# The V chunk of the differential heads projected before the other heads' q and k, in a hybrid attention layer

## Chip, cores and metric

The kernel runs on one core of a Trainium2 chip. The metric is the device time of one execution in microseconds (us), the median of several runs of the same program.

## What is computed

One decoder layer for 256 tokens of width 1024, all in float32. One input projection gives q, k and v of two groups of heads: four differential heads (two softmaxes each, the second subtracted with a weight) and eight block-sparse heads, which at 256 tokens see one causal block each. One output projection mixes both, then follow a layer norm, a SwiGLU feed-forward and a second layer norm.

```
proj = x @ w_in
dq, dk, dv, mq, mk, mv = split(proj)          # 512 columns each
# differential heads: q, k as 4 heads x 2 x 64, v as 4 heads x 128
p = softmax(causal(rope(dq) @ rope(dk).T / 8))
a = p[:, :, 0] - lam * p[:, :, 1]
o = a @ dv;  o = o * rsqrt(mean(o*o) + eps) * subln_g * (1 - lambda_init)
# the other 8 heads of 64: one block of 256, its own
b = softmax(causal(rope(mq) @ rope(mk).T / 8)) @ mv
x = layer_norm(alpha * x + concat(o, b) @ w_o)
f = (silu(g) * u) @ w_ffn_out                 # g, u = split(x @ w_ffn_in)
x = layer_norm(alpha * x + f)
```

## The kernel before

Each product of two float32 matrices is made of three matmuls on rounded parts: a matrix is split into `hi` (a cast on ScalarE, line 108) and `lo` (what is left, a subtraction on VectorE, line 109), and `mm3` (line 155) adds hi*hi, hi*lo and lo*hi. Weights come in units of 128 x 4 x 512 (four blocks of 512): units 0 to 11 are the six chunks of the input projection, two units each, 12 to 15 the output projection, then the feed-forward. A unit is loaded whole or in parts by SyncE into one of four raw buffers, and split into one of four hi and four lo buffers. `spread` (line 126) lays the splits of coming units over the steps of a projection, in `pieces` parts a unit: at 4, one block of 512 at a time.

The chunks stand in the order q and k of the differential heads (0, 1), q and k of the other heads (2, 3), V of the differential heads (4), V of the others (5). `proj_qkT` (line 422) makes a q or k chunk transposed, in 32 steps of three matmuls of 256 columns; at the end of a chunk's first half `rope` rotates it (a shuffle, two products, later an addition and the split, `finish`), at the end of its second half `plain` splits the rest. `proj_v` (line 454) makes a V chunk in 16 steps of three matmuls of 512 columns and copies it out on ScalarE.

Other work is hooked onto steps of the projections; the tables of lines 38 to 40 name the steps. `scores(g, b)` (line 305) makes the scores of four heads into four PSUM banks, then reduces them on VectorE (line 319) and takes the exponentials on ScalarE (line 322). `diff_combine` (line 336) subtracts the two softmaxes on VectorE (line 344), `diff_pt` transposes the result on TensorE and copies it on ScalarE, `diff_pv` (line 350) multiplies with V and normalises: VectorE (line 365), eight squares on ScalarE (line 367), a power on GpSimd (line 370), VectorE (line 371). `diff_mix` transposes that into the first half of `mixh`, `mixl`. For the other heads `norm1` and `moba_norm` scale the exponentials (VectorE and ScalarE), `moba_pt` transposes them, `moba_pv` multiplies with V and fills the second half. `wo(t, n, half)` (line 500) is a quarter of the output projection over one half of the mix, 12 matmuls of 512 columns. Behind the attention the buffers are closed, and GpSimd's queue loads the norm's rows (`load_rows`, line 527) into the space that comes free.

Before, the two scores of group 0 are hooked into chunk 2 (steps 15 and 28), the combine into chunk 3 (step 12), its transposes into chunk 3 (steps 22, 25, 28, 31), the scores of group 1 into chunk 4 (steps 5 and 11). Chunk 5 carries `diff_pv` (step 4), `norm1` (5), six of the eight `moba_pt` (8 to 13) and both `diff_mix` (12 and 14).

A hook is the earliest place in program order, not a fixed one. A planner walks the program when it is built, with times of its own, and puts on each engine's queue the first instruction in program order that it takes to be ready; on the chip each queue then runs in that order and waits where an input is late. `run` (line 293) also puts VectorE's instructions of a hook behind the last reduction of the scores traced so far.

## Time and profile before

| | |
|---|---|
| median of 3 runs | 309.2 us (309.18 to 309.55) |
| the profiled execution | 309.19 us |
| its span in the trace | 307.4 us |
| TensorE busy | 296.7 us, 97% of the span |
| VectorE busy | 246.6 us, 80% |
| ScalarE busy | 181.2 us, 59% |
| DMA | 57.25 MB, mean 186 GB/s |

The span runs from the first instruction to the last; 1.8 us of the execution lie around it. A busy share is a mean over stages: here the attention with its projections (up to about 118 us) is one part and the feed-forward the rest. An engine that is marked busy may still be held inside an instruction, so starts are compared with starts.

### The profile page before, as it was taken

Reading aid. Unit: us, or ns where it says so; the run is one execution under the profiler, and the core shown is the slowest. Engines: PE = TensorE matmul, PEld = TensorE weight load, DVE = VectorE, ACT = ScalarE, POOL = GpSimd, SP = SyncE. Lnnn points to the kernel's source line nnn. Section 1 sums busy time; section 2 is a strip of 40 time slices with the busy share of each in tenths; the row PEclk is TensorE's granted clock in tenths of the full one; section 3 lists DMA queues with packets and bytes.
Section 4 is the critical chain, followed back from the end, with each engine's and each line's share of the span. In section 5 each row is a group of like instructions: output and inputs, shape, how many; then the busy total and the mean of one; then the engine's idle time right before and its main releaser. Section 6 shows DMA issues by size and latency. Waiting matters only on the chain.

```text
span 307.4 us, 4877 instructions
## 1 busy us (share of the span) xinstructions
PE 296.7 (97%) x1835; PEld 254.4 (83%) x1835; DVE 246.6 (80%) x460; ACT 181.2 (59%) x349; POOL 9.0 (3%) x18
## 2 busy tenths in 40 slices
PE   8999999899999999999999999999999999999990
PEld 5899998878886888888888888888888888888890
DVE  3697999977684489849598797598768999997995
ACT  4684888587994326357466567547747746557000
POOL 1000000000110011000000000000000000000011
PEclk9999999999999999999999999999999999999997
DMA  6988984345359243529554664574470365824011
GB/s 187 338 271 270 418 341 146 135 148 194 122 201 310 116 139 128 199 85 330 216 160 141 247 194 140 215 241 151 156 245 31 107 211 194 309 91 184 0 68 68
DMA packets 14390, 57.25 MB, mean 186 GB/s; under 512 B 1760, under 2 KB 2784, under 8 KB 9632
## 3 DMA queue, kind: packets, MB, share of 16 engines
q1 hardware_dynamic: 14080, 54.86, 51.6%
q0 software_dynamic: 288, 2.10, 1.7%
q8 instruction: 14, 0.23, 0.3%
q14 instruction: 8, 0.07, 0.1%
HBM read 55.90 MB, written 1.05 MB: 185 GB/s over the span
## 4 chain that ended last, share of the span: by engine, by line
PE 88%; DVE 6%; DMA 2%; SPq 1%; issue 1%; ACT 0%; DVEq 0%
PE fc L681 22%; PE foc L757 12%; PE fc L682 11%; PE pj L156 6%; PE pj L158 6%; PE pj L157 6%; PE fo L757 5%; PE wo L156 3%; PE fr L157 2%; PE fr L156 2%; PE wo L157 2%; PE wo L158 2%; PE fr L158 2%; DMA xTr<-in_xT_dram 2%; DVE lo L109 2%; PE s L314 2%
## 5 line engine op out<-in xcount | busy, mean ns | idle before, releaser
L109 DVE TENSOR_TENSOR lo<-raw,hi 128x512 fp32r<-128x512 f32 (+2 forms) x114 | 104.0, 938 | 21.4 <-ACT hi L108 21.1
L108 ACT CAST hi<-raw 128x512 fp32r<-128x512 f32 (+2 forms) x114 | 88.9, 824 | 21.5 <-PE wo L158 9.9
L681 PE MATMUL fc<-x1T,hi 128*128 128x512 f32 x288 | 100.1, 392 | 0.0
L682 PE MATMUL fc<-x1T,lo 128*128 128x256 f32 x288 | 80.5, 280 | 0.0
L681 PEld LDWEIGHTS fc<-x1T,hi 128*128 128x128 f32 x288 | 54.1, 188 | 11.9
L682 PEld LDWEIGHTS fc<-x1T,lo 128*128 128x128 f32 x288 | 54.0, 188 | 0.0
L156 PE MATMUL pj<-xTh,hi 128*128 128x256 f32 x128 | 36.5, 292 | 0.1
L158 PE MATMUL pj<-xTh,lo 128*128 128x256 f32 x128 | 36.0, 286 | 0.3
L157 PE MATMUL pj<-xTl,hi 128*128 128x256 f32 x128 | 36.0, 283 | 0.0
L684 ACT COPY v<-fc 128x256 f32<-128x256 f32 x36 | 13.3, 368 | 22.0 <-PE fc L682 21.9
L156 PEld LDWEIGHTS pj<-xTh,hi 128*128 128x128 f32 x128 | 24.3, 192 | 1.4 <-ACT hi L218 1.2
L158 PEld LDWEIGHTS pj<-xTh,lo 128*128 128x128 f32 x128 | 24.1, 190 | 1.2 <-DVE lo L220 0.8
L157 PEld LDWEIGHTS pj<-xTl,hi 128*128 128x128 f32 x128 | 24.3, 190 | 0.0
L685 DVE TENSOR_TENSOR v<-v,fc 128x256 f32<-128x256 f32 x36 | 15.0, 417 | 6.2 <-ACT v L684 6.2
L757 PE MATMUL foc<-lo,hTh 128*128 128x512 f32 x46 | 18.2, 395 | 0.0
L757 PE MATMUL foc<-hi,hTh 128*128 128x512 f32 x46 | 18.1, 394 | 0.0
L757 PE MATMUL foc<-hi,hTl 128*128 128x512 f32 x46 | 18.1, 394 | 0.0
L322 ACT ACTIVATE E<-E,negm 128x128 f32<-128x128 f32 (+1 forms) x32 | 14.1, 443 | 4.3 <-DVE negm L319 4.3
L156 PE MATMUL pj<-hi,xTh 128*128 128x512 f32 x32 | 13.5, 422 | 0.0
L156 PE MATMUL wo<-hi,mixh 128*128 128x512 f32 x32 | 12.9, 404 | 0.0
L688 ACT ACTIVATE v<-v 128x256 f32<-128x256 f32 x18 | 7.5, 419 | 9.1 <-DVE v L685 9.1
L156 PE MATMUL fr<-hi,x1T 128*128 128x512 f32 x32 | 12.9, 402 | 0.0
(190 smaller groups left out, 517.9 us busy)
## 6 DMA issues: line engine op xcount, KB each, us to landing
raw<-in_w_f_dram SPq DMA_DIRECT2D x27, 1024.0 KB, 5.1
raw<-in_w_in_dram SPq DMA_DIRECT2D x24, 256.0 KB, 6.0
raw<-in_w_in_dram SPq DMA_DIRECT2D x4, 1024.0 KB, 8.2
raw<-in_w_o_dram SPq DMA_DIRECT2D x4, 1024.0 KB, 4.8
raw<-in_w_f_dram SPq DMA_DIRECT2D x12, 256.0 KB, 3.7
raw<-in_w_f_dram SPq DMA_DIRECT2D x6, 512.0 KB, 4.5
raw<-in_w_in_dram SPq DMA_DIRECT2D x4, 512.0 KB, 7.3
rows<-in_rows_dram POOLq DMA_DIRECT2D x2, 1024.0 KB, 6.4
```

The costliest lines, as they stand in the source:

```text
L108: nc.scalar.copy(h, src)
L109: nc.vector.tensor_sub(l, src, h.bitcast(F32))
L156: nc.tensor.matmul(ps, sh, mh, start=first, stop=False)
L157: nc.tensor.matmul(ps, sh, ml, start=False, stop=False)
L158: nc.tensor.matmul(ps, sl, mh, start=False, stop=last)
L322: nc.scalar.activation(e, e, AF.Exp, bias=negm[g][:, i, u : u + 1], scale=-1.0, accum_out=ls[g][:, i, u : u + 1])
L681: nc.tensor.matmul(ps, hi[u][:, i, ws], x1T[:, k], start=k == 0, stop=False)
L682: nc.tensor.matmul(ps[:, 0, :], lo[u][:, i, ws], x1T[:, k, 0, :], start=False, stop=k == KT - 1)
L684: nc.scalar.copy(v, ps[:, 1, :])
L685: nc.vector.tensor_add(v, v, ps[:, 0, :])
L688: nc.scalar.activation(gate, gate, AF.Silu)
L757: nc.tensor.matmul(bank[name] if ps is None else ps, x, w[:, cs], start=key not in opened, stop=last and (m, i) == (len(todo) - 1, 2))
```

## The change

The V chunk of the differential heads (4) now stands third: chunks 0, 1, 4, 2, 3, 5. The units are numbered in that order. Its projection carries the two scores of group 0 (steps 7 and 14) and the finish of k's rotation. Chunk 2 carries the combine (step 20) and its own rotation's finish (24, before 31). Chunk 3 carries the differential transposes (2, 5, 8, 11) and `diff_pv` (24). Chunk 5 carries both `diff_mix` (0 and 1) and the scores of group 1 (4 and 10). `norm1` with its scalings and all eight `moba_pt` stand behind chunk 5, between quarters of the output projection; the third quarter, `wo(1, 0, 0)`, moves ahead of the last two `moba_pv`. In `spread`, units of chunks 4 and 5 and of the output projection go in 2 pieces (two blocks at a time), those of q and k in 4.

```diff
--- before.py
+++ after.py
@@ -35,9 +35,12 @@
 SPLIT_PIECES = {16: 4, 17: 4, 18: 4, 19: 4}
 
 
-FIN0, FIN1, FIN2, FIN3 = (20, 26), (4, 7), 31, 20
-SCORES0, SCORES1 = (15, 28), (5, 11)
-COMBINE, DIFF_PT = 12, (22, 25, 28, 31)
+FIN0, FIN1, FIN2, FIN3 = (20, 26), (2, 4), 24, 20
+SCORES0, SCORES1 = (7, 14), (4, 10)
+COMBINE, DIFF_PT, DIFF_PV = 20, (2, 5, 8, 11), 24
+
+
+ORDER = (0, 1, 4, 2, 3, 5)
 
 
 
@@ -68,7 +71,7 @@
 
 
     units = []
-    for c in range(6):
+    for c in ORDER:
         for h in range(2):
             units.append(w_in[c, :, 4 * h : 4 * h + 4, :])
     for u in range(4):
@@ -99,7 +102,7 @@
 
     def split(u, r, s):
         h, l = hi[u][:, s, :], lo[u][:, s, :]
-        if u < 8:
+        if u < 12 and ORDER[u // 2] < 4:
 
             src = r[:, s, :].rearrange("p i (h t d) -> p i t h d", t=2, d=32)
             h, l = (v.rearrange("p i (t h d) -> p i t h d", t=2, d=32) for v in (h, l))
@@ -125,12 +128,14 @@
 
     def spread(units_, pieces, steps):
 
-        gens = [(u, p) for u in units_ for p in range(pieces)]
+
+        pieces = {u: pieces if u < 12 and ORDER[u // 2] < 4 else 2 for u in units_}
+        gens = [(u, p) for u in units_ for p in range(pieces[u])]
         live = {}
 
         def emit(u):
             if u not in live:
-                live[u] = split_gen(u, pieces)
+                live[u] = split_gen(u, pieces[u])
                 state["split"] = u + 1
             next(live[u])
 
@@ -415,7 +420,7 @@
 
 
     def proj_tok(ps, c, t, k):
-        u, i = 2 * c + k // 4, k % 4
+        u, i = 2 * ORDER.index(c) + k // 4, k % 4
         ts_ = slice(t * P, (t + 1) * P)
         mm3(ps, xTh[:, k, ts_], xTl[:, k, ts_], hi[u][:, i, :], lo[u][:, i, :], k == 0, k == KT - 1)
 
@@ -426,14 +431,15 @@
         kb = {0: 1, 1: 4}.get(c, KT)
         order = [(j, k0 + k) for k0 in range(0, KT, kb) for j in range(4) for k in range(kb)]
         fin = []
-        ahead(2 * c, splits=-1)
-        bg = spread([1] + [2] if c == 0 else [3, 4, 5] if c == 1 else [2 * c + 2, 2 * c + 3], 4, 28)
+        u0 = 2 * ORDER.index(c)
+        ahead(u0, splits=-1)
+        bg = spread([1] + [2] if c == 0 else [3, 4, 5] if c == 1 else [u0 + 2, u0 + 3], 4, 28)
         for n, (j, k) in enumerate(order):
             if n == 16:
-                ahead(2 * c + 1, splits=-1)
+                ahead(u0 + 1, splits=-1)
             for f in side.get(n, []) + bg.get(n, []):
                 run(f)
-            u, i = 2 * c + k // 4, k % 4
+            u, i = 2 * ORDER.index(c) + k // 4, k % 4
             ws = slice(j * P, (j + 1) * P)
             ps = pss[j][:, 0, :] if c < 2 else pss[j // 2][:, j % 2, :]
             mm3(ps, hi[u][:, i, ws], lo[u][:, i, ws], xTh[:, k, :], xTl[:, k, :], k == 0, k == KT - 1)
@@ -454,11 +460,12 @@
     def proj_v(c, side):
 
         pss = [psA.tile([P, 512], F32, tag="acc", name=f"pj{c}_{t}") for t in range(2)]
-        ahead(2 * c, splits=-1)
-        bg = spread([2 * c + 2, 2 * c + 3], 4, 14)
+        u0 = 2 * ORDER.index(c)
+        ahead(u0, splits=-1)
+        bg = spread([u0 + 2, u0 + 3], 4, 14)
         for n, (t, k) in enumerate((t, k) for t in range(2) for k in range(KT)):
             if n == 8:
-                ahead(2 * c + 1, splits=-1)
+                ahead(u0 + 1, splits=-1)
             for f in side.get(n, []) + bg.get(n, []):
                 run(f)
             proj_tok(pss[t], c, t, k)
@@ -473,26 +480,28 @@
     sc = {FIN1[i]: [f] for i, f in enumerate(fin)}
     for b in range(2):
         sc.setdefault(SCORES0[b], []).append(lambda b=b: scores(0, b))
-    proj_qkT(2, sc)
-    sc = {COMBINE: [diff_combine]}
+    proj_v(4, sc)
+    proj_qkT(2, {COMBINE: [diff_combine]})
+    sc = {}
     for h in range(4):
         sc.setdefault(DIFF_PT[h], []).append(lambda h=h: diff_pt(h))
+    od = {}
+
+    def run_diff_pv():
+        od["o"] = diff_pv()
+
+    sc[DIFF_PV] = [run_diff_pv]
     proj_qkT(3, sc)
     alloc_group(1)
-    proj_v(4, {SCORES1[b]: [lambda b=b: scores(1, b)] for b in range(2)})
-    od = {}
-
-    def run_diff_pv():
-        od["o"] = diff_pv()
+    sd = {i: [lambda i=i: diff_mix(i, od["o"][i])] for i in range(2)}
+    for b in range(2):
+        sd[SCORES1[b]] = [lambda b=b: scores(1, b)]
+    proj_v(5, sd)
 
     def norm1():
         nc.vector.reciprocal(rl[1], ls[1])
-
-    sd = {4: [run_diff_pv], 5: [norm1] + [lambda u=u: moba_norm(u) for u in range(8)],
-          12: [lambda: diff_mix(0, od["o"][0])], 14: [lambda: diff_mix(1, od["o"][1])]}
-    for n, u in enumerate(range(6)):
-        sd.setdefault(8 + n, []).append(lambda u=u: moba_pt(u))
-    proj_v(5, sd)
+        for u in range(8):
+            moba_norm(u)
 
 
     acc = [[psA.tile([P, 512], F32, tag="acc", name=f"wo{t}_{n}") for n in range(2)] for t in range(2)]
@@ -505,12 +514,16 @@
             mm3(acc[t][n], mixh[:, e, ts_], mixl[:, e, ts_], hi[u][:, i, :], lo[u][:, i, :], e == 0, e == 7)
 
     ahead(12, splits=3)
+    run(norm1)
     wo(0, 0, 0)
+    for u in range(4):
+        moba_pt(u)
+    wo(0, 1, 0)
     moba_pv(0)
-    moba_pt(6)
-    moba_pt(7)
     moba_pv(1)
-    wo(0, 1, 0)
+    for u in range(4, 8):
+        moba_pt(u)
+    wo(1, 0, 0)
     moba_pv(2)
     moba_pv(3)
     axT.close()
@@ -567,7 +580,6 @@
         nc.scalar.copy(x1T_h[:, ks, ts_], pt)
         nc.vector.tensor_sub(x1T_l[:, ks, ts_], pt, x1T_h[:, ks, ts_].bitcast(F32))
 
-    wo(1, 0, 0)
     ahead(12)
     wo(0, 0, 1)
     ln_part("a", 0, 0, x_sb, acc[0][0])
```

## Rows read from the trace of the kernel before

**Rows 1.** The page: part 1, busy time of the engines; part 4, the chain by engine.

```profile
PE 296.7 (97%) x1835; PEld 254.4 (83%) x1835; DVE 246.6 (80%) x460; ACT 181.2 (59%) x349; POOL 9.0 (3%) x18
...
PE 88%; DVE 6%; DMA 2%; SPq 1%; issue 1%; ACT 0%; DVEq 0%
```

**Rows 2.** Table by stage; columns: us, PE, PEld, DVE, ACT, POOL busy (x), PEclk, DMA, GB/s.

```profile
29.90:45.20 15.30, 15.30 (x195) 14.70 (x194) 15.23 (x49) 12.77 (x37) 0.00 (x0) 1.00 0.98 401
45.20:59.80 14.60, 13.07 (x110) 12.70 (x110) 14.60 (x44) 10.20 (x31) 0.00 (x0) 1.00 0.43 145
59.80:74.40 14.60, 14.60 (x146) 11.80 (x145) 10.74 (x43) 11.31 (x41) 0.00 (x0) 1.00 0.41 145
74.40:91.10 16.70, 16.70 (x99) 14.24 (x98) 12.38 (x26) 16.51 (x46) 2.48 (x2) 1.00 0.47 156
91.10:103.90 12.80, 12.80 (x76) 9.52 (x75) 5.20 (x8) 4.83 (x9) 0.71 (x1) 1.00 0.80 290
```

**Rows 3.** Timeline, PE, chunk 3; columns: start us, us, engine, line, op, tiles, form, idle.

```profile
52.75 0.28 PE L157 MATMUL pj<-xTl,hi 128*128 128x256 f32 x1
52.87 0.28 PE L158 MATMUL pj<-xTh,lo 128*128 128x256 f32 x1
...
54.67 0.30 PE L327 MATMUL ppd<-ident,E 128*128 128x128 f32 x1 [1.52 <-DVE E L344]
...
56.57 0.36 PE L156 MATMUL pj<-xTh,hi 128*128 128x256 f32 x1
56.77 0.27 PE L157 MATMUL pj<-xTl,hi 128*128 128x256 f32 x1
```

**Rows 4.** Timeline, VectorE, 39 to 57 us: first softmax, reciprocal, the combine.

```profile
39.75 0.29 DVE L319 CUSTOM_DVE_ANT_0 E<-s,mask 128x128 f32<-128x128 f32 x1
...
41.99 0.74 DVE L270 STREAM_SHUFFLE sh<-pj 128x512 f32<-128x512 f32 x1
...
52.05 0.24 DVE L339 RECIPROCAL rl<-ls 128x16 f32<-128x16 f32 x1
...
54.19 2.70 DVE L344 SCALAR_TENSOR_TENSOR E<-E,sc 128x128 f32<-128x128 f32 x8
```

**Rows 5.** Timeline, PE, the first eight matmuls of the two scores of group 0.

```profile
38.12 0.51 PE L314 MATMUL s<-h,h 32*128 32x256 f32 x8
...
41.74 0.87 PE L314 MATMUL s<-h,h 32*128 32x256 f32 x8
```

**Rows 6.** Timeline, ScalarE: first and last instruction of the second score's exponentials.

```profile
45.95 0.40 ACT L322 ACTIVATE E<-E,negm 128x128 f32<-128x128 f32 x1 [0.16 <-DVE negm L319]
...
49.38 0.19 ACT L322 ACTIVATION_READ_ACCUMULATOR E<-E,negm 128x1 f32 x1
```

**Rows 7.** Timeline, VectorE, pieces of weights: four of 512 and two of 1024 in a row.

```profile
67.22 2.49 DVE L109 TENSOR_TENSOR lo<-raw,hi 128x512 fp32r<-128x512 f32 x4
...
92.88 2.36 DVE L109 TENSOR_TENSOR lo<-raw,hi 128x1024 fp32r<-128x1024 f32 x2 [0.64 <-ACT hi L108]
```

**Rows 8.** Timeline, VectorE, the second half of the differential output, from dpv to od.

```profile
80.07 0.69 DVE L365 TENSOR_TENSOR od<-dpv,rl 128x512 f32<-128x512 f32 x1 [0.83 <-PE dpv L358]
...
86.97 0.69 DVE L371 TENSOR_TENSOR od<-od,ff 128x512 f32<-128x512 f32 x1 [1.13 <-POOL ff L370]
```

**Rows 9.** Timeline, ScalarE: scaling of seven E, two copies of transposes, two casts of 1024.

```profile
76.79 2.90 ACT L386 ACTIVATE E<-E,rl 128x256 f32<-128x256 f32 x7
...
85.27 0.84 ACT L331 COPY ptm<-ppm 128x384 f32<-128x384 f32 x2
...
91.80 2.00 ACT L108 CAST hi<-raw 128x1024 fp32r<-128x1024 f32 x2
```

**Rows 10.** Waits: engine, what, released by: us in total, times, longest us.

```profile
POOL rows L529 <- PE ppm L329: 9.1, 1, 9.1
```

**Rows 11.** The page, part 6: DMA, engine op xcount, KB, us from issue to landing.

```profile
rows<-in_rows_dram POOLq DMA_DIRECT2D x2, 1024.0 KB, 6.4
```

**Rows 12.** Timeline, VectorE: first step of the layer norm that reads the rows.

```profile
111.35 1.40 DVE L555 SCALAR_TENSOR_TENSOR x<-z,mva,rows 128x512 f32<-128x512 f32 x2
```

More of the change, by code (lines that the diff above doesn't have):

```diff
@@ L475, in hybrid_layer_kernel @@
         sc.setdefault(SCORES0[b], []).append(lambda b=b: scores(0, b))
-    proj_qkT(2, sc)
-    sc = {COMBINE: [diff_combine]}
+    proj_v(4, sc)
+    proj_qkT(2, {COMBINE: [diff_combine]})
+    sc = {}
     for h in range(4):
         sc.setdefault(DIFF_PT[h], []).append(lambda h=h: diff_pt(h))
-    proj_qkT(3, sc)
-    alloc_group(1)
-    proj_v(4, {SCORES1[b]: [lambda b=b: scores(1, b)] for b in range(2)})
     od = {}
@@ L486, in run_diff_pv @@
         od["o"] = diff_pv()
+    sc[DIFF_PV] = [run_diff_pv]
+    proj_qkT(3, sc)
+    alloc_group(1)
+    sd = {i: [lambda i=i: diff_mix(i, od["o"][i])] for i in range(2)}
+    for b in range(2):
+        sd[SCORES1[b]] = [lambda b=b: scores(1, b)]
+    proj_v(5, sd)
     def norm1():
         nc.vector.reciprocal(rl[1], ls[1])
-    sd = {4: [run_diff_pv], 5: [norm1] + [lambda u=u: moba_norm(u) for u in range(8)],
-          12: [lambda: diff_mix(0, od["o"][0])], 14: [lambda: diff_mix(1, od["o"][1])]}
-    for n, u in enumerate(range(6)):
-        sd.setdefault(8 + n, []).append(lambda u=u: moba_pt(u))
-    proj_v(5, sd)
+        for u in range(8):
+            moba_norm(u)
     acc = [[psA.tile([P, 512], F32, tag="acc", name=f"wo{t}_{n}") for n in range(2)] for t in range(2)]
```

## Prediction

> **What bounds the kernel now.** I read the page first. TensorE is busy 97% of the span, and the chain that ended last is TensorE for 88%, VectorE for 6% [rows 1]. So nothing that merely makes VectorE or ScalarE lighter counts; only time in which TensorE's queue stands still counts. The table by stage tells where that can be: the stretch 45.2 to 59.8 us, which is chunk 3, is the only one in which TensorE is not busy throughout (13.07 of 14.60), and VectorE is busy there without a break, as in the stage ahead of it (15.23 of 15.30) [rows 2]. The timeline names the place. Matmuls of 256 columns start every 0.12 us; the one at 52.87 should be followed at 52.99, but the first transpose of the differential heads starts at 54.67, released by the combine on VectorE: **1.68 us** [rows 3]. On VectorE the combine began only at 54.19, although the reciprocal that it needs was done at 52.3 and the exponentials ahead of it at 49.6 [rows 4, 6]: it stood behind other work. A smaller wait lies in the second score of group 0: its first eight matmuls take 0.87 us where the first score's took 0.51, so 0.36 us for PSUM banks that the first softmax still holds [rows 5]. The other large stall of the trace is the start, which the change doesn't touch. TensorE's work itself stays: the same matmuls in another order. About 2.0 us are thus to be had in this part, and the rest of the forecast is what the new order puts in their place.
>
> **The wait at the combine.** Before, 10 steps of chunk 3 (3.6 us at three matmuls of 0.12) lie between combine and first transpose; after, 14 steps (12 of chunk 2, two of chunk 3, 5.0 us). The rotation of a q or k chunk, six passes of about 0.6 us on VectorE (one is the 0.74 at 41.99 [rows 4]), no longer stands between the two softmaxes of group 0, because a V chunk has none. My ledger of VectorE: chunk 4 starts at 29.9 like chunk 2 did and takes 14.6 us with its two scores, as it does now in the third stage [rows 2], plus the 0.4 us wait: end 44.9. The first score can't run earlier than now (38.12 [rows 5]), since the rotation of k and the same pieces of weights come ahead of it on VectorE. Its softmax takes 2.2 us (39.75 to 41.99 [rows 4]). Unit 7 follows, 2.4 us by four pieces [rows 7], then the second softmax, to about 46.6. The exponentials take 3.6 us (45.95 to 49.57 [rows 6]) and end at about 48.3. From there VectorE has, ahead of the first head's combine: unit 8 2.4, half of unit 9 1.2, three passes of the rotation 1.9, reciprocal and two small ones 0.5, the first pair of the combine 0.7 (2.70 for eight [rows 4]): 6.7 us, so 55.0 even if none of it was done earlier. Chunk 2 ends at 44.9 + 11.5 = 56.4, and step 2 of chunk 3 comes at 57.1. The margin is 2.1 us; the term is **-1.68**. What is late next on VectorE are the last two blocks of unit 9, wanted at step 6 of chunk 3 (58.5) and due at 58.2 behind the rest of the combine (1.9) and these two (1.2): close, but the planner can take another column block first. Zero, with 0.5 as upper end.
>
> **The wait at the second score** stays in my sum. The first score is held to 38.1, near step 12, the second is hooked at step 14, so the banks are as tight as before: bounds -0.36 and +0.5, value 0, as the same two instructions meet.
>
> **Two blocks at a time.** Four pieces of 512 take 2.49 us on VectorE, two of 1024 take 2.36 [rows 7]: 0.13 a unit, 0.8 over units 4, 5 and 10 to 13. It is off TensorE's path: 0. The price would be that a piece waits for two loads while the DMA engines are full (0.98 of the first stage [rows 2]). But a V chunk wants its second unit at step 4, 2.8 us in, where a q or k chunk wanted it 1.4 us in. That covers it; without the cover it would cost one block's pass, 0.6 us.
>
> **Transposes in groups.** Behind three transposes the next matmul start comes after 0.20 instead of 0.12 us (56.57 to 56.77 [rows 3]). Six groups of transposes that stood singly in chunk 5 become two runs of four: four returns less, **-0.3** (bounds 0 and -0.5).
>
> **The differential output.** From the second product to its normalised result 7.6 us pass now (80.07 to 87.66 [rows 8]), and nobody waits, as `diff_mix` is hooked far behind. Now `diff_pv` is followed by eight steps (2.9 us), a `diff_mix` (0.4) and one step of chunk 5 (0.7): 4.0 us. On TensorE's queue the transposes would hold chunk 5's matmuls, and behind those the scores of group 1. Bounds: 0, since the chain's two VectorE passes are only 1.4 us of it and ScalarE is lighter in chunk 3 than in chunk 5 (10.20 of 14.60 against 16.51 of 16.70 [rows 2]); and 3.6, if the chain stays at 7.6. The planner may set the transposes behind later matmuls, as it set the first score, hooked at step 15 of chunk 2 (35.2 us), at 38.12, where it didn't wait [rows 5]. So only the planner's error is paid. I take **+0.4**, nearer to the score than to the 1.68 of the combine.
>
> **Behind chunk 5.** This is the weak point. ScalarE's 4.83 us of the stage 91.1 to 103.9 [rows 2] grow by eight scalings (seven in 2.90), six copies of transposes (two in 0.84) and perhaps unit 14's casts (2.00) [rows 9]: to some 12.6 us. TensorE's 12.8 us [rows 2] grow by six groups of transposes to 14.8. ScalarE also enters the stage without air, since chunk 5 gets the exponentials of group 1 (twice 3.6 [rows 6]) for what it gives away. The chain is strict: scaling, transpose, copy, product with V, cast, and `wo(0, 0, 1)` wants all four products; `wo(1, 0, 0)`, which covered their casts, now stands ahead of the last two. If TensorE's queue follows the text, the transposes come 2.8 us behind chunk 5 (12 matmuls at 0.23), while the first scaled E comes behind V's copy, two units' casts (4.0) and one scaling, at about 5.0: a wait of 2.2 to 2.4. If the planner puts `wo(0, 1, 0)` and `wo(1, 0, 0)` ahead, 5.6 us of cover, it is 0. Value **+0.5**, for the planner's error.
>
> **GpSimd's queue.** The load of the norm's rows waits for the last transposes of the other heads [rows 10], which come some 5 us later behind chunk 5, at about 98.5. With 6.4 us to land [rows 11] and an issue of about 1, the rows are there at 106, and their first reader starts at 111.35 now [rows 12], some 1 to 2 us earlier then. Zero, 3 us of cover. SyncE's queue keeps its order of loads.
>
> **The sum.** 309.19 us of the profiled execution (307.4 of span and 1.8 around it, and equal to the median of 309.2): -1.68 - 0.3 + 0 + 0.4 + 0.5 = -1.1, so **308.1 us**. From about 118 us on TensorE runs without a gap before, so what is gained or lost by then stays.
>
> **Rivals.**
> 1. *All of it, no new wait.* The planner fills both new places with matmuls that are ready. 309.19 - 1.98, and with the PSUM wait gone too -2.34: 306.8 to 307.5. For it speaks how well the first score was placed [rows 5]; against it the 1.68 us that the same planner misjudged at the combine [rows 3].
> 2. *A new wait in place of the old one.* Either VectorE is as late for the transposes as it was, so that the change doesn't do what it says (its softmaxes, rotations and splits are the same work), or the two new waits come to 1.5 to 2.3 us, about the 1.68 of the combine each time in part: 308.6 to 309.8. For it: ScalarE full in chunk 5 (16.51 of 16.70 [rows 2]) and a chain of 7.6 us in 4.0 [rows 8]. Against it: the ledger's 2.1 us of margin.
> 3. *Slower, by ScalarE behind chunk 5.* The transposes of the scaled E stand in TensorE's queue where the text has them, ScalarE comes out of chunk 5 late, and its 12.6 us run as one chain with the products. It decides from the point where the first scaled E comes more than about 4 us behind the end of chunk 5 with only one quarter of the output projection ahead of its transposes. Price 2.4, with up to 1 of lateness from chunk 5, and the casts of the last two products, no longer covered, 0.7: 309.19 - 1.98 + 3.4 to 4.1 = 310.6 to 311.3; with half of the lateness 309.9. For it: six of eight transposes were done inside chunk 5 before; against it: two quarters of ready work, which the planner sees.
> 4. *The clock.* The granted clock stayed at 1.00, which is 2.4 GHz, through the stage with the 1.68 us wait [rows 2]. By the Trainium skill, "TensorE: Matmul & The Clock Gate" (section "Part 1: The HAM clock gate"), an array that has been idle is clocked at half, 1.2 GHz, until it has been busy again. That rule speaks against an order that gathers waits in one place: on top of rival 3, one quarter of the output projection at half the clock would cost 2.8 us more (an estimate from 12 matmuls at 0.23), 313 to 314. No wait in this trace behind the start brought the clock down, and the ones that I expect are shorter.
>
> **How the numbers follow.** Forecast (307.5 to 308.6) 0.40, rival 1 0.21, rival 2 0.19, rival 3 0.18, rival 4 0.02. A measurement of this kernel tells 0.2%, 0.6 us, from no change: the bounds are 308.6 and 309.8. Faster is the forecast but for a tail of 0.01 and rival 1: 0.60; the same is rival 2 and that tail: 0.20; slower are rivals 3 and 4: 0.20. The range leaves out the upper half of rival 3 and rival 4, about 0.1, and below it little: 306.7 to 310.2.
>
> **What would show it.** In the profile after: the first transpose of the differential heads (line 327) starts 0.1 us behind the matmul ahead of it, with no idle time by line 344. VectorE has short gaps between chunk 4 and chunk 3. The transposes of `diff_mix` (line 378) and of the scaled E (line 327) show what they waited for: VectorE at line 371, and line 385 or ScalarE at line 386; up to 0.5 us each is my case, 2 us or more at the latter is rival 3. TensorE's stages sum to the same work. I am wrong if TensorE waits at a place that I held covered: for weights of chunk 4 or chunk 3, for PSUM ahead of the second score by over 0.5 us, or for the norm's rows.

## The result and the profile after

The changed kernel is slower: a median of 311.07 us (309.31 to 313.11, 19 executions) against 309.05 (308.09 to 309.66, 19) of the kernel before on the same chip, ratio 1.0071 [1.0053, 1.0089]. The forecast was 308.1, the range 306.7 to 310.2. The profiled execution of after is one of its quicker ones: 309.75 us, span 308.0.

The loss has two parts, which the list of all executions tells apart. Each execution has a mean granted clock of TensorE. Those of after (31, with a second series of the same kernel) fall into groups with nothing between them; those of before (72, run beside the experiments below) are all in the upper one.

| mean granted clock | after, executions | us | before, executions |
|---|---|---|---|
| 0.991 and above | 15 | median 309.8 (309.1 to 310.5) | 72 (308.1 to 310.4) |
| 0.987, 0.988 | 10 | 310.8 to 311.7 | 0 |
| 0.983 | 6 | 311.9 to 313.5 | 0 |

Executions at 0.991 and above are called undisturbed below. So a part is lost in these too, by waits that the profile shows: 0.5 us in the first series (their median is 309.6, against 309.05) and 1.2 in the second (310.1 against 308.9). The rest of the median of 311.07, 1.5 us, comes from the 13 of 19 executions in which the mean clock was lower; in both series together these were 16 of 31.

The page of after: busy time by engine, and the chain that ended last by engine.

```profile
PE 296.8 (96%) x1835; PEld 255.6 (83%) x1835; DVE 245.8 (80%) x448; ACT 180.1 (58%) x337; POOL 8.6 (3%) x18
...
PE 83%; DVE 8%; ACT 4%; DMA 1%; issue 1%; POOL 1%; DVEq 0%; SPq 0%; POOLq 0%
```

TensorE's work is what it was (296.7 in [rows 1]). Its share of the chain went from 88% to 83%; VectorE, ScalarE and GpSimd took over what it gave up. The table by stage of after (us, busy time and count of PE, PEld, DVE, ACT, POOL; PEclk, DMA share, GB/s): chunks 4, 2, 3, 5, and the stage behind chunk 5.

```profile
29.70:44.40 14.70, 14.70 (x146) 11.95 (x145) 14.36 (x45) 13.26 (x35) 0.00 (x0) 1.00 0.96 393
44.40:55.80 11.40, 11.40 (x97) 11.36 (x96) 10.43 (x33) 8.03 (x25) 0.00 (x0) 1.00 0.72 258
55.80:71.50 15.70, 15.55 (x134) 15.34 (x132) 12.68 (x21) 9.50 (x26) 1.03 (x1) 1.00 0.41 149
71.50:89.30 17.80, 16.56 (x153) 13.37 (x154) 12.18 (x43) 12.85 (x43) 1.02 (x1) 1.00 0.19 61
89.30:104.30 15.00, 14.83 (x94) 11.41 (x92) 7.85 (x17) 12.52 (x27) 0.71 (x1) 1.00 0.72 245
```

The gap of before stood in chunk 3, where TensorE had 13.07 of 14.60 and VectorE no break [rows 2]. That stage now has 15.55 of 15.70, and VectorE has room in it. The new gap is in chunk 5: 16.56 of 17.80. The timeline of TensorE in after shows the old place, mended: the transpose follows the matmul ahead of it at 0.12 us.

```profile
56.42 0.28 PE L163 MATMUL pj<-xTh,lo 128*128 128x256 f32 x1
56.54 0.27 PE L332 MATMUL ppd<-ident,E 128*128 128x128 f32 x1
```

And the new one, TensorE in after at the start of chunk 5 (start, us, engine, line, operation, tiles, form, idle time and what ended it).

```profile
71.07 0.28 PE L163 MATMUL pj<-xTh,lo 128*128 128x256 f32 x1
71.68 0.63 PE L383 MATMUL dm<-ident,od 128*128 128x128 f32 x4 [0.33 <-DVE od L376]
...
75.17 0.40 PE L162 MATMUL pj<-lo,xTh 128*128 128x512 f32 x1
75.85 0.63 PE L383 MATMUL dm<-ident,od 128*128 128x128 f32 x4 [0.28 <-DVE od L376]
76.41 0.51 PE L319 MATMUL s<-h,h 32*128 32x256 f32 x6
...
76.99 0.28 PE L319 MATMUL s<-l,h 32*128 32x256 f32 x2
78.04 0.38 PE L319 MATMUL s<-h,h 32*128 32x256 f32 x1 [0.78 <-DVE mixl L386]
...
79.56 0.50 PE L163 MATMUL pj<-hi,xTl 128*128 128x512 f32 x1
```

By starts: `diff_mix(0)` should have come at 71.19 and came at 71.68, **0.49 us**; `diff_mix(1)` at 75.40 and came at 75.85, **0.45**. Then the score that follows serves six of its first eight matmuls, which is three of its four banks, and stands for **1.05** until 78.04. The row names what ended it: not an input of the score, but `mixl` (line 386), the last reader of the bank that `diff_mix(1)` had just written. The price is larger than the time it stands. Of its 48 matmuls, 14 had started ahead of the wait; the 34 that were left, with those of the late bank on their own at first, take 1.52 us, about what a score that waits for nothing takes for all 48 (1.53). From its start to the next matmul of the projection the score takes 3.15 us, **1.62** more than such a score. A fourth, smaller wait is behind chunk 5, where a transpose that should start at 93.46 waits 0.33 for the scaled E on ScalarE:

```profile
93.23 0.39 PE L161 MATMUL wo<-hi,mixh 128*128 128x512 f32 x1
93.79 0.33 PE L333 MATMUL ppm<-ident,E 128*128 128x128 f32 x1 [0.17 <-ACT E L391]
```

The chain behind the second wait can be followed through three engines of after: VectorE, ScalarE and GpSimd, from the second product with V to the bank's release.

```profile
68.55 0.69 DVE L370 TENSOR_TENSOR od<-dpv,rl 128x512 f32<-128x512 f32 x1 [0.88 <-PE dpv L363]
...
71.45 2.35 DVE L112 TENSOR_TENSOR lo<-raw,hi 128x1024 fp32r<-128x1024 f32 x2
73.72 0.16 DVE L374 TENSOR_SCALAR ss<-ss 128x4 f32<-128x4 f32 x1
...
75.02 0.69 DVE L376 TENSOR_TENSOR od<-od,ff 128x512 f32<-128x512 f32 x1 [0.54 <-POOL ff L375]
...
77.24 0.75 DVE L386 SCALAR_TENSOR_TENSOR mixl<-dm,gsub,mixh 128x512 fp32r<-128x512 f32 x1 [0.87 <-ACT mixh L385]
```
```profile
70.19 1.03 ACT L111 CAST hi<-raw 128x1024 fp32r<-128x1024 f32 x1
...
71.43 1.03 ACT L111 CAST hi<-raw 128x1024 fp32r<-128x1024 f32 x1
72.36 0.31 ACT L372 ACTIVATE sq<-od 128x128 f32<-128x128 f32 x1
```
```profile
73.96 1.02 POOL L375 TENSOR_TENSOR ff<-ss,mhalf 128x4 f32<-128x4 f32 x1 [3.15 <-DVE ss L374]
```

From 68.55 to the end of line 376 at 75.71 are 7.2 us, about as in before (7.6 [rows 8]): two casts of weights stand between the squares on ScalarE, two pieces of weights hold `ss` on VectorE (from 71.45), and the power on GpSimd takes 1.02. Then transposes, `mixh`, `mixl` add 2.3 us until the bank is free.

### The profile page after: what moved, and what is told of

The parts are those of the page before. It is cut to its first block, busy times and chain, and to the rows that moved or that the text cites. A ratio compares the mean times of both kernels' runs of the same rounds, so it can differ in the third digit from the quotient of the medians.

```text
span 308.0 us, 4849 instructions
## 1 busy us (share of the span) xinstructions
PE 296.8 (96%) x1835; PEld 255.6 (83%) x1835; DVE 245.8 (80%) x448; ACT 180.1 (58%) x337; POOL 8.6 (3%) x18
## 3 DMA queue, kind: packets, MB, share of 16 engines
HBM read 55.90 MB, written 1.05 MB: 185 GB/s over the span
## 4 chain that ended last, share of the span: by engine, by line
PE 83%; DVE 8%; ACT 4%; DMA 1%; issue 1%; POOL 1%; DVEq 0%; SPq 0%; POOLq 0%
PE fc L693 21%; PE foc L769 12%; PE fc L694 11%; PE fo L769 5%; PE pj L161 5%; PE pj L163 5%; PE pj L162 5%; DVE lo L112 3%; PE fr L161 2%; PE fr L162 2%; PE fr L163 2%; PE s L319 2%; PE wo L163 2%; PE wo L162 2%; PE wo L161 2%; ACT E L327 1%
## 5 line engine op out<-in xcount | busy, mean ns | idle before, releaser
L112 DVE TENSOR_TENSOR lo<-raw,hi 128x1024 fp32r<-128x1024 f32 (+2 forms) x102 | 102.3, 1031 | 21.0 <-ACT hi L111 20.8
L111 ACT CAST hi<-raw 128x1024 fp32r<-128x1024 f32 (+2 forms) x102 | 87.0, 897 | 23.6 <-PE wo L163 10.2
L162 PE MATMUL pj<-xTl,hi 128*128 128x256 f32 x128 | 36.7, 287 | 0.0
```

Source lines behind the costliest of these rows:

```text
L111: nc.scalar.copy(h, src)
L112: nc.vector.tensor_sub(l, src, h.bitcast(F32))
L162: nc.tensor.matmul(ps, sh, ml, start=False, stop=False)
```

## Experiments

A measure used below is the stage from the first matmul behind chunk 1 (the 193rd of the projections) to the first matmul of the feed-forward, by starts on TensorE: 88.73 us in before, 89.52 in after. It leaves out the start, which differs by up to 1.4 us between traces, and what follows, which differs by at most 0.3. Each trace is one execution. Ratios are against the kernel before on the same chip, with 95% intervals.

**Series a_again: after once more.**

> The changed kernel itself, once more. Its times so far lie in groups with the mean granted clock: 309.3 to 310.1 us at 0.991 to 0.996, 310.8 to 311.7 at 0.987 to 0.988, 311.9 to 313.1 at 0.983. Theory CLOCK: in most executions TensorE falls to 1.2 GHz for one or two stretches in the sparse part at the start of chunk 5 (72 to 80 us: the transposes of diff_mix that wait, the scores that wait for PSUM); the trace of such an execution shows the granted clock at 0.5 there, and the matmuls behind it start at 0.46 instead of 0.23 us. Theory WAITS: the extra time is a longer wait in some executions (loads, VectorE) at a granted clock of 1.00 throughout; the trace then shows one wait of 1 to 3 us more. Median 311 by both.

310.14 us (309.13 to 313.52), ratio 1.0046 [1.0023, 1.0069]. Three of its 12 executions were at 0.983 to 0.987, against 13 of 19 in the first series. The loss is there again, and how often the clock falls differs from series to series.

**Run a_mix_late: only `diff_mix` moved back, to steps 12 and 14 of chunk 5, behind the scores, as before had it.**

```diff
-    sd = {i: [lambda i=i: diff_mix(i, od["o"][i])] for i in range(2)}
+    sd = {12 + 2 * i: [lambda i=i: diff_mix(i, od["o"][i])] for i in range(2)}
```

> The changed kernel with diff_mix at steps 12 and 14 of chunk 5, as in the kernel before, instead of 0 and 1. Both waits of TensorE for the normalised differential output (0.49 and 0.45 us in the trace) and the wait of the scores for PSUM behind them (1.05) should go. Theory WAITS: 2.0 us less, median about 309.0. Theory CLOCK: these 2.0 us and the lowered clock too, so no execution over 310 and a median of 307.2 to 307.6, with the mean clock at 0.99 or more in every execution. If the clock falls somewhere else (the scores of group 0, the part behind chunk 5), times up to 311 remain.

307.30 us (306.74 to 308.88), ratio 0.9955 [0.9938, 0.9972]; the stage 87.13, which is 2.4 less than in after; all clocks at 0.992 and above. TensorE in this kernel:

```profile
73.87 0.51 PE L319 MATMUL s<-h,h 32*128 32x256 f32 x8
...
75.41 0.50 PE L161 MATMUL pj<-hi,xTh 128*128 128x512 f32 x1
...
82.60 0.40 PE L163 MATMUL pj<-hi,xTl 128*128 128x512 f32 x1
82.84 0.60 PE L383 MATMUL dm<-ident,od 128*128 128x128 f32 x4
```

All eight first matmuls of the score run at once, in 0.51 us as the first score of group 0 did [rows 5], the whole score takes 1.53, and the transposes follow without a wait, after 0.24 us (the second ones, at 84.67, after 0.23). One line turns a loss into a gain: the place of `diff_mix` is the cause of the waits. It is that of the lower clock too: in the four kernels of the new order in which `diff_mix` stands behind the first score of group 1 (this one, and a_mix_six, a_mix_four and a_mix_norm below) the lower clock was seen in none of 40 executions; after had it in 16 of 31.

**Run a_mix_six: `diff_mix` at steps 6 and 7**, where its inputs are ready, but ahead of the second score of group 1. It separates the wait for inputs from the wait for the bank.

```diff
-    sd = {i: [lambda i=i: diff_mix(i, od["o"][i])] for i in range(2)}
+    sd = {6 + i: [lambda i=i: diff_mix(i, od["o"][i])] for i in range(2)}
```

> The changed kernel with diff_mix at steps 6 and 7 of chunk 5, that is behind the first scores of group 1 (step 4) instead of ahead of them. Theory: the waits at diff_mix and for PSUM come from its place ahead of the scores alone; the normalised output is there by 75.7 us, before step 6 (about 76.5), so nothing waits: 307.3 us as with steps 12 and 14. Rival: its two PSUM banks now hold up the second scores (step 10) or ScalarE takes its cast late: up to 1 us more.

308.19 us (307.63 to 308.65), ratio 0.9973 [0.9959, 0.9986]. TensorE, the transposes and the second score of group 1:

```profile
77.70 0.40 PE L163 MATMUL pj<-hi,xTl 128*128 128x512 f32 x1
77.94 0.60 PE L383 MATMUL dm<-ident,od 128*128 128x128 f32 x4
...
80.56 0.60 PE L319 MATMUL s<-h,h 32*128 32x256 f32 x5
81.43 0.39 PE L319 MATMUL s<-h,h 32*128 32x256 f32 x2 [0.27 <-DVE mixl L386]
```

Nothing waits at the transposes, yet the score starts with five of its eight matmuls, and stands until `mixl` has read the bank; it takes 2.40 us instead of 1.53. The expected 307.3 was missed, and the rival named beside it came true. The stage is 87.70, 0.6 more than with `diff_mix` behind the scores. The bank is a wait of its own.

**Run a_pv_late: `diff_pv` at step 30 instead of 24**, so that the chain starts later and the waits grow.

```diff
-COMBINE, DIFF_PT, DIFF_PV = 20, (2, 5, 8, 11), 24
+COMBINE, DIFF_PT, DIFF_PV = 20, (2, 5, 8, 11), 30
```

> The changed kernel with diff_pv at step 30 of chunk 3 instead of 24: the waits at diff_mix grow, since 2.1 us less lie between the product with V and the transposes. Theory CLOCK: the clock falls in nearly every execution, so the trace shows a granted clock of 0.5 in a stretch at the start of chunk 5 and matmuls of 512 columns at 0.46 us there; time 311.5 to 315. Theory WAITS: the granted clock stays at 1.00 and the time grows by no more than the longer waits, 1 to 2 us, to 311 to 312.

314.05 us (311.75 to 315.27), ratio 1.0157 [1.0119, 1.0194]. The waits were 1.32, 0.87 and 1.05 us. Three of four executions were at a mean clock of 0.98, the profiled one (313.58) among them. So here the fallen clock can be seen in place: the table by stretches and the timeline of TensorE of this kernel.

```profile
77.60:81.05 3.45, 1.95 (x22) 1.24 (x21) 1.45 (x2) 0.69 (x1) 0.21 (x1) 1.00 0.02 5
81.05:87.88 6.83, 6.83 (x61) 5.58 (x65) 3.45 (x17) 4.08 (x17) 0.00 (x0) 0.50 0.00 0
87.88:91.00 3.12, 3.12 (x46) 2.65 (x43) 2.11 (x15) 1.78 (x9) 0.00 (x0) 1.00 0.02 5
```
```profile
84.52 0.63 PE L162 MATMUL pj<-lo,xTh 128*128 128x512 f32 x1
84.94 0.63 PE L163 MATMUL pj<-hi,xTl 128*128 128x512 f32 x1
```

For 6.83 us the granted clock is 0.50, which is 1.2 GHz, and matmuls of 512 columns start every 0.43 us instead of 0.23. In the stretch ahead TensorE had worked 1.95 of 3.45 us: two of the three waits, and transposes and scores of 32 rows between them. The clock fell right behind the third wait, the one for the bank, which ended at 80.88. The rest of this score, the seven matmuls of the projection behind it and the second score took some 3 us more than as many of the same kinds took in after.

**Runs a_fill and a_pv_fill: after and a_pv_late with matmuls that nobody reads, hooked beside `diff_mix` and ahead of the score.**

```diff
-    sd = {i: [lambda i=i: diff_mix(i, od["o"][i])] for i in range(2)}
+    fill = {}
+
+    def keep(n):
+        if "ps" not in fill:
+            fill["ps"] = psA.tile([P, 512], F32, tag="acc", name="fill")
+        for _ in range(n):
+            nc.tensor.matmul(fill["ps"], warm[:, :P], warm, start=True, stop=True)
+
+    def keep_behind_mix():
+        nc.tensor.matmul(fill["ps"], od["o"][1][:, 0, :], V[0][:, 0, :], start=True, stop=True)
+
+    sd = {0: [lambda: keep(2), lambda: diff_mix(0, od["o"][0])],
+          1: [lambda: diff_mix(1, od["o"][1]), keep_behind_mix]}
...
+    sd[SCORES1[0]].insert(0, lambda: keep(2))
```

(a_pv_fill: `keep(5)` and `keep(3)` ahead of the two `diff_mix`.)

> The changed kernel with five matmuls added whose result nobody reads: two of 512 columns in bf16 ahead of the first transposes of diff_mix, and behind the second ones a float32 product of 512 columns that reads the same input as they do (0.9 us) and two more in bf16. They stand where TensorE waits (0.49 us and 1.05 us in the trace) and should fill these waits rather than lengthen anything. Theory CLOCK: with the stretch filled the clock no longer falls; all executions at a mean clock of 0.99 or more, and the median goes down from 310 to 311 to about 309.7, although work was added. Theory WAITS: the same distribution as the changed kernel or up to 0.5 us more.

> The variant with diff_pv at step 30, in which the granted clock fell to 0.5 from 81.1 to 87.9 us (time 313.6; four executions, three at a mean clock of 0.98), with matmuls added whose result nobody reads: five of 512 columns in bf16 ahead of the first transposes of diff_mix, three ahead of the second, one float32 product and two in bf16 behind them. They lie where TensorE waits (1.3, 0.9 and 1.05 us). Theory CLOCK by idle time: filled, the clock stays up in all executions, and the time falls to 311 to 312 with more work on TensorE. Rival, that the sparse matmuls themselves (scores on 32 rows, transposes) bring the clock down: falls remain in most executions, 313 to 315.

a_fill: 310.30 us (309.54 to 310.59), ratio 1.0046 [1.0028, 1.0064]; a_pv_fill: 312.83 (312.71 to 312.94), ratio 1.0126 [1.0110, 1.0142]. All ten executions are at 0.992 and above, and their spread is 1.1 and 0.2 us, where after's was 3.8 and a_pv_late's 3.5. TensorE in a_pv_fill:

```profile
71.28 1.25 PE L502 MATMUL fill<-warm 128*128 128x512 bf16 x5
...
72.59 0.40 PE L162 MATMUL pj<-lo,xTh 128*128 128x512 f32 x1
74.21 0.63 PE L383 MATMUL dm<-ident,od 128*128 128x128 f32 x4 [1.22 <-DVE od L376]
...
78.14 0.40 PE L163 MATMUL pj<-hi,xTl 128*128 128x512 f32 x1
79.26 0.63 PE L383 MATMUL dm<-ident,od 128*128 128x128 f32 x4 [0.73 <-DVE od L376]
79.73 1.02 PE L505 MATMUL fill<-V,od 128*128 128x512 f32 x2
...
81.11 0.84 PE L319 MATMUL s<-h,h 32*128 32x256 f32 x8
```

The waits for `od` are still there, 1.39 and 0.90 us, and empty: the planner set the matmuls that need no input (71.28 and 74.92) well ahead of them. Only the third wait is filled: the product that reads `od` and two more matmuls stand between the transposes and the score, which then has its banks for all eight first matmuls. In a_fill it is the same: a wait for `od` of 0.93 us stays ahead of the second transposes, and the one for the bank is filled. The median of a_pv_fill is 1.2 us below that of a_pv_late (on another chip; the intervals overlap). What went with the filling is the empty wait at the bank and the fallen clock. It is no remedy: neither comes to before's time, a_fill is not under the undisturbed executions of after (309.8; 309.7 was expected), and a_pv_fill (311 to 312 was expected) is above the one undisturbed execution of a_pv_late, 311.75.

**Run a_four: after with every unit in four pieces. Run b_two: before with two pieces from unit 8 on.** Each is the second part of the change alone, taken away or added.

```diff
-        pieces = {u: pieces if u < 12 and ORDER[u // 2] < 4 else 2 for u in units_}
+        pieces = {u: pieces for u in units_}
```
```diff
-        gens = [(u, p) for u in units_ for p in range(pieces)]
+        pieces = {u: pieces if u < 8 else 2 for u in units_}
+        gens = [(u, p) for u in units_ for p in range(pieces[u])]
...
-                live[u] = split_gen(u, pieces)
+                live[u] = split_gen(u, pieces[u])
```

> The changed kernel with every unit split one block at a time, that is without its second part. Theory of the prediction: the pieces are off TensorE's path, 0.8 us more on VectorE, no difference in time (within 0.3 us of the changed kernel). Rival: the larger pieces hold up the small steps on VectorE and ScalarE between dpv and diff_mix (pieces of 1.1 us lie there in the trace), so with small pieces the waits at diff_mix fall by up to 1 us and the time by 0.5 to 1.5 us.

> The kernel before with the second part of the change alone: units of the V chunks and of the output projection two blocks at a time. Theory of the prediction: 0, within 0.3 us of the kernel before. Rival: VectorE has 0.4 us less ahead of the combine or small steps wait longer, which moves the 1.68 us wait at the first transpose by up to 0.5 either way.

a_four: 311.35 us (310.31 to 312.00), ratio 1.0081 [1.0059, 1.0103], the stage 90.60, 1.1 longer than after's. The waits at `diff_mix` are 1.26 and 0.78 us (0.49 and 0.45 in after), although the score behind them stands only 0.36 for its banks and takes 2.22. TensorE in a_four:

```profile
71.43 0.28 PE L163 MATMUL pj<-xTh,lo 128*128 128x256 f32 x1
72.81 0.63 PE L383 MATMUL dm<-ident,od 128*128 128x128 f32 x4 [1.10 <-DVE od L376]
...
74.91 0.40 PE L162 MATMUL pj<-lo,xTh 128*128 128x512 f32 x1
75.92 0.63 PE L383 MATMUL dm<-ident,od 128*128 128x128 f32 x4 [0.61 <-DVE od L376]
```

All six executions were at 0.991 and above. b_two: 309.77 (308.36 to 310.87), ratio 1.0018 [1.0000, 1.0036]; five of its 12 executions were at 0.988, the other seven have a median of 309.0 (before on this chip: 308.9). Its trace, in which the clock had not fallen, has the wait of [rows 3] grown from 1.68 to 2.05:

```profile
52.30 0.28 PE L159 MATMUL pj<-xTh,lo 128*128 128x256 f32 x1
54.47 0.30 PE L328 MATMUL ppd<-ident,E 128*128 128x128 f32 x1 [1.89 <-DVE E L345]
```

So the two-block pieces alone bring nothing in the old order, and in the new one they are worth some 1 us.

**Run a_mix_four: a_mix_late with four pieces everywhere**, the new order without either disturbance.

> The changed kernel with diff_mix at steps 12 and 14 and every unit split one block at a time. Against the same with two blocks (307.3 us) it gives the price of the two-block pieces when nothing waits at diff_mix. Theory of the prediction: within 0.3 us. Rival: ScalarE and VectorE behind chunk 5 are late by their longer pieces' sum (0.8 us of VectorE, 1 us of ScalarE), 308.

308.69 us (307.30 to 310.31), ratio 0.9995 [0.9977, 1.0012]; the stage 87.80 against 87.13. TensorE, the second score of group 0:

```profile
41.86 0.80 PE L319 MATMUL s<-h,h 32*128 32x256 f32 x6
...
42.72 0.38 PE L319 MATMUL s<-h,h 32*128 32x256 f32 x1
```

The score stands twice for PSUM banks of the first softmax, 0.30 and 0.33 us, and from its start to the next matmul of chunk 4 takes 2.38 us where after took 1.70. The planner had set the first score behind 36 matmuls of chunk 4 (33 in after) and left six between the two scores (nine in after), so the first softmax had less time. Without the two-block pieces the new order gains nothing, even with `diff_mix` at a good place.

**Run a_mix_norm: a_mix_late with `norm1` ahead of the last splits behind chunk 5**, which brings the scaling of E earlier on ScalarE. If ScalarE behind chunk 5 cost much, this would show it.

```diff
-    ahead(12, splits=3)
     run(norm1)
+    ahead(12, splits=3)
     wo(0, 0, 0)
```

> The changed kernel with diff_mix at steps 12 and 14, and with the scaling of the other heads' exponentials ahead of the splits of units 14 and 15 behind chunk 5. The planner then sets the first four transposes of the scaled exponentials ahead of the first quarter of the output projection. Theory of rival 3 of the prediction: TensorE then waits there until ScalarE has taken the last exponentials and scaled the first, 1.5 to 2.5 us, and the time is 309 to 310. Theory that the 0.31 us wait at these transposes comes from the casts of unit 15 alone: it goes, 307.0.

307.52 us (307.27 to 307.67), ratio 0.9954 [0.9937, 0.9970], the same as a_mix_late's. The wait at the transposes (0.31 there) is gone, and one of 0.28 has come at the product with V, at 94.93. There is no long wait behind chunk 5 to be had back.

**Runs b_pt_late and b_pt_scores: the old order, with nothing but step numbers changed.** If the gain of the change is the 1.68 us alone, later transposes should bring it without moving a chunk.

```diff
-COMBINE, DIFF_PT = 12, (22, 25, 28, 31)
+COMBINE, DIFF_PT = 12, (28, 29, 30, 31)
```

b_pt_scores has this, and the scores at (15, 30) and (7, 12) instead of (15, 28) and (5, 11).

> The kernel before with the four transposes of the differential heads at steps 28 to 31 of chunk 3 instead of 22, 25, 28 and 31: nothing else is moved. The combine ended its first pair at 54.7 us, step 28 comes at about 55.1. Theory, that the gain of the new order is the 1.68 us wait at the first transpose: it goes here too, 307.3 to 307.6 us. Rival: the wait moves to the next consumer (the last transposes, the product with V or the scores of chunk 4), 308 to 309.

> The kernel before with the differential transposes at steps 28 to 31 of chunk 3 and, besides, the second scores of group 0 at step 30 of chunk 2 (28 before) and the scores of group 1 at steps 7 and 12 of chunk 4 (5 and 11 before). With the transposes alone moved, the trace shows two waits left behind the start: 0.34 us at the second scores of group 0 (PSUM) and 0.34 us at the first scores of group 1 (the last part of k on VectorE). Theory: both go, 306.6 to 306.9 us. Rival: the later scores push softmax and combine back by 0.7 us, and the transposes at step 28 wait again: 307.3 to 307.6.

b_pt_late: 307.33 us (306.86 to 308.20), ratio 0.9952 [0.9936, 0.9968]; the first transpose has no wait any more:

```profile
54.47 0.28 PE L158 MATMUL pj<-xTh,lo 128*128 128x256 f32 x1
54.59 0.27 PE L327 MATMUL ppd<-ident,E 128*128 128x128 f32 x1
```

Two waits of 0.34 are left in its stage, at the second score of group 0 and at the first of group 1. b_pt_scores takes both away: **306.66 us** (306.10 to 307.19), ratio 0.9933 [0.9919, 0.9946]. It beats both kernels; against a_mix_late and b_pt_late the intervals overlap. The new order of chunks isn't needed for the gain.

## Why the prediction was wrong, step by step

The sum of the prediction beside the undisturbed execution in the trace:

| step | predicted | measured |
|---|---|---|
| wait at the combine | -1.68 | -1.93 (0.25 of it behind the first transpose) |
| wait at the second score | 0 | -0.19 |
| transposes in groups | -0.3 | 0, nothing to be had |
| `diff_mix`, waits for its input | +0.4 | +0.94 (0.49 and 0.45) |
| `diff_mix`, its PSUM bank | not in the sum | +1.62 (1.05 of it standing still) |
| behind chunk 5 | +0.5 | +0.33 |
| two-block pieces | 0 | in the rows above |
| sum | -1.1 | +0.77 by these rows, +0.79 by the stage |

The stage grew by 0.79 us, the undisturbed executions by 0.5 and 1.2 in the two series.

**The combine** went as the ledger said: chunk 4 ended at 44.44 (44.9 forecast), the transposes came at 56.54 (57.1), without a wait. A little more was to be had than the 1.68: in before the transposes behind the first were late as well, 54.67, 54.98 and 55.14 by starts, where 0.11 us apart is usual. The second of them in before, and the last transpose of the second group, which is used further down:

```profile
54.98 0.33 PE L328 MATMUL ppd<-ident,E 128*128 128x128 f32 x1
...
56.54 0.27 PE L329 MATMUL ppd<-ident,E 128*128 128x128 f32 x1
```

a_mix_late is the change without the step that failed, and its 307.30 lies where rival 1 put it (306.8 to 307.5).

**The step that failed is the differential output.** Two things were wrong in it. The size first: of two rows to lean on I took the first score, which the planner had placed well [rows 5], and not the 1.68 us that it had misjudged [rows 3]. The planner put `diff_mix(0)` where the text has it, behind 24 matmuls of chunk 3, and `diff_mix(1)` behind 14 matmuls of chunk 5 instead of three; the chain took 7.2 us, and both were late, by 0.94 together, more than twice the value. The larger one is the **bank**. The text says that "the transposes would hold chunk 5's matmuls, and behind those the scores of group 1", which follows only the transposes' input. Their output takes one of the four banks of a pool that a score wants whole, and it is free only when ScalarE and then VectorE have read it. The rows to see it were there: [rows 5] shows a score that waits for banks held by another reader. The term was left out, and it measured 1.62 us, 1.05 of them standing still. a_mix_six shows such a cost alone: 0.87 us, with no wait at the transposes.

**The pieces** were put at 0, and in before's order that is what b_two gave beside the clock. In the new order it was wrong, to the other side: by a_mix_four and a_four the pieces are worth 0.7 to 1.1 us. The 0.13 us a unit that I priced is not what they bring. They go with another choice of the planner: with them it sets the first score three matmuls sooner, and the second score takes 1.70 us instead of 2.38. Without them the change would have come out worse still. Why the waits at `diff_mix` grow with four pieces was not followed further.

**Transposes in groups**: the -0.3 rests on a reading of [rows 3] that leaves out the row ahead. The last of the three transposes starts at 56.54, the next matmul of the projection already at 56.57, and only the one behind it comes 0.20 later: together 0.23 us, twice the usual 0.12. The return costs nothing, so nothing could be saved by grouping. The planner didn't keep the groups either: it set some of these transposes in twos between matmuls of `wo`.

**Behind chunk 5** the value held (0.33 for 0.5). Rival 3 did not happen: the scaling at line 391 started at 93.23, 3.9 us behind the end of chunk 5, just short of the 4 us from which it was to decide, and the planner had a quarter of the output projection and part of the next in between. a_mix_norm found nothing to be had there. The price that the prediction gives rival 3 "with half of the lateness", 309.9, doesn't follow from its own terms, which give 310.1 without the casts and 310.8 with them. Rival 2 is the nearest to the traced execution of after, 309.75 us inside its 308.6 to 309.8. But it reckons with 1.5 to 2.3 us of new waits, and 2.9 were measured, 1.62 of them at a place that it did not name; that the time still fits is in part luck, since 2.1 us went instead of 1.68. The median of all executions is outside.

**GpSimd's rows**: the load was issued at 101.15 (98.5 forecast), took 6.0 to land, and its first reader started at 111.93: the cover held, 4.8 us.

**The clock** was rival 4, with a chance of 0.02, tied to rival 3 and to a place behind chunk 5. That the clock could fall was right; the place and the condition were not. The reason for the low chance, that the waits I expected were shorter than the 1.68 us which had left the clock at 1.00 [rows 2], failed: no wait of after is that long, but three stand within 7 us, with transposes and scores of 32 rows between. The Trainium skill, "TensorE: Matmul & The Clock Gate", section "A second HAM failure mode: psum-queue depth-cycling", tells of a kernel in which TensorE idles briefly between groups of matmuls, often enough that the clock goes back and forth between its two levels. The trace of a_pv_late agrees in part: the clock fell behind waits of 1.32, 0.87 and 1.05 us, but once, for 6.83 us, and no run here shows it going back and forth. The prediction drew on the section on an idle array alone.

What is shown of it and what is not: the lower clock and its price per execution are measured, in after 1.0 to 1.9 us for the 0.987 group and 2.1 to 3.7 for the 0.983 one (against 309.8); that the place of `diff_mix` brings the fall is shown by moving it (0 of 40 executions against 16 of 31); that it falls at these waits is seen in a_pv_late alone. No execution of after with the fallen clock was traced, so its place there is inferred, and in b_two, which has no `diff_mix` ahead of the scores, it is not known. Which of the three waits matters is open. The runs point at the last: after and a_pv_late, where TensorE stands 1.05 us for the bank behind two waits for `od`, have the fall; a_four (1.26 and 0.78 us for `od`, 0.36 for banks, six executions) and the two filled kernels (waits for `od` left, the bank's filled, ten executions) don't. No run changed the bank's wait and nothing else, so this is not shown.

## What to carry to other kernels

When a step moves ahead of another, follow its output as well as its inputs: which PSUM bank or buffer it takes, who must read it before it is free, and whether the next step on the queue needs that bank. Before a large reordering, try the step numbers: the wait that this change removed went when the four transposes moved to steps 28 to 31. And look at the granted clock of every execution, not of the profiled one alone: a median can carry a cost that the trace at hand doesn't have.

## What the runs showed of the hardware

- The same kernel, unchanged, came out at 309.1 to 313.5 us with two traces that show nothing of it; the mean granted clock sorts the times into groups (309.8, 310.8 to 311.7, 311.9 to 313.5).
- In before a single wait of 1.68 us never brought the clock under 0.991 in 72 executions; with 2.05 us in its place (b_two) it was 0.988 in 5 of 12, and those took 0.9 to 1.9 us more than the median of the others. Where in b_two it fell was not traced.
- Unread matmuls in the wait for the bank went with a clock at 0.992 and above in 10 of 10 executions, though waits for `od` of up to 1.39 us stayed empty, and the kernel with more TensorE work was no slower (312.83 against 314.05).
- A score whose last bank came late cost more than it stood still: 1.05 us of standing, 3.15 us instead of 1.53 for its 48 matmuls.
- Three transposes between matmuls of 256 columns cost their own 0.11 us each and no return: the next two matmuls start 0.03 and 0.20 us on, where two usual steps are 0.23.
